# Zeros beside the low parts of the queries, and an exponential written into the tile of weights

## The chip, the core and the metric

The kernel runs on one core of a Trainium2 chip. A core has five engines, each with an instruction queue of its own that it works through in order: TensorE (PE in the profile, its weight loads are PEld), VectorE (DVE), ScalarE (ACT), GpSimd (POOL) and SyncE (SP, which issues the DMAs). They wait for each other by semaphores. The metric is the device time of one launch in microseconds, the median of some runs. Beside the times there is one profiled execution, whose trace has every instruction with its start and its duration.

## The reference

Two layers over 528 positions (16 learned ones ahead of 512) and 1024 channels in float32. The first is a Hyena mixer (long convolutions), the second a differential attention with 16 heads; each ends with a norm and a residual. The change lies in the second. Cut to what matters:

```python
def diff_attention_mixer(h, w_in, lam_vecs, subln, w_out, cos, sin, layer_idx):
    u = h @ w_in
    # q, k: (B, T, 16 heads, 2 maps, 64), turned by the rotary tables; v: (B, T, 16, 128); z: the gate
    def attend(qb):
        s = jnp.einsum("bqhmd,bkhmd->bhmqk", qb, k).astype(F32) * scale
        p = jax.nn.softmax(s, axis=-1)
        p = p[:, :, 0] - lam * p[:, :, 1]
        return jnp.einsum("bhqk,bkhd->bqhd", p.astype(v.dtype), v)
    o = rmsnorm(o, subln, DA_NORM_EPS) * (1.0 - lam_init)
    return (o.reshape(B, T, D_INNER) * jax.nn.silu(z)) @ w_out
```

Each head has two maps of scores over 64 dimensions. Their softmaxes are subtracted, and the difference weighs the values.

## The kernel before

Float32 products are made of three: each operand is split into a high part that the fast float32 format of TensorE holds exactly and the low rest, and high x high, high x low and low x high are summed in PSUM.

**The scores of a tile.** The 512 queries of a head are four tiles of 128, so the layer has 64 tiles; I count them through, tile 0 to 63, tile 4 being the first of the second head. `scores` makes one tile. A map has 64 dimensions and the array 128 rows, so two of the three products fit into one passage: `ks[:, map]` holds the high part of the keys on its own 64 partitions and the low part on the other 64, and `qs[:, map]` holds the high part of the queries on both. One matmul of line 1302 for each half of the 528 keys (264 columns) makes high x high and high x low. The third product, low queries x high keys, is line 1306: `ql` holds the low parts of map 0 on partitions 0 to 63 and of map 1 on 64 to 127, and each matmul takes the 64 partitions of its map alone. So a tile has four matmuls of line 1302 and four of line 1306. A map's scores lie in a PSUM tile `a` of two banks, of which there are two.

**From scores to weights.** Line 1309 is VectorE's maximum over the 528 scores of a query, line 1311 ScalarE's exponential with its sum. Both exponentials go to tiles `E`, of which there are three. Line 1317 is VectorE's sum `E0 - factor x E1` into the tile of weights `pp`. There are eight of these, four for a head. Line 1318 is a copy by GpSimd of the weights of the 16 learned positions, line 1327 the transposes of the weights (four transposes of 128 keys for each of four tiles of keys, and one group with 96 columns for the 16 learned positions), lines 1348 to 1352 weights x values. The pool of `pp` also serves the first layer's result, which `turn_back` (line 966) copies out of PSUM and sends to DRAM at the start of the attention for the last residual.

**What sets the order.** `attend` writes the four tiles of scores of a head and, between them, the transposes and weighted values of the head before. Between those it issues steps of a list of projections (`Filler`): keys, queries, values and gates of later heads (lines 345, 348 and 1189) and output projections of earlier ones (line 1237). A scheduler then puts each engine's instructions into a final order by a simulated timeline of its own, so the order on the engines is not that of the source. The reading of tile buffers (pools with a number of buffers) sets further waits: whoever writes a buffer waits for the last reader of what was in it. `q_split` (line 1139) makes `qs` and `ql` out of a head's turned queries.

Of the kernel before, what the change touches and what calls it, by code (L numbers as in the profile page):

```python
# [10 lines left out]
F32 = mybir.dt.float32  # L11
F32R = mybir.dt.float32r
I32 = mybir.dt.int32
AF = mybir.ActivationFunctionType
# [5 lines left out]
P = 128  # L20
# [16 lines left out]
# ---------------------------------------------------------------- host side  # L37
# [95 lines left out]
# -------------------------------------------------------------- device side  # L133
# [7 lines left out]
class Item:  # L141
    """one projection: its weight tiles in DRAM, and its steps as (cost, body)"""
# [5 lines left out]
class Filler:  # L148
    """Steps of projections in their order; they are issued between the steps of the chains that
    would leave the tensor engine waiting, their weights one item ahead."""  # L150
# [42 lines left out]
class Trunk:  # L193
# [20 lines left out]
    def rsqrt(self, dst, src, scale, eps, n, rows=P):  # L214
        """dst = (src * scale + eps) ** -0.5 on small tiles."""
# [17 lines left out]
    def root(self, dst, src, scale, eps, n, rows=P):  # L233
        """dst = (src * scale + eps) ** -0.5 by the square root of ScalarE and one step of Newton's"""
# [13 lines left out]
    def token_rms(self, part, tiles, scale=1.0 / D, how=None):  # L248
        """1/rms of tiles of tokens, from sums of squares over the channels: one column for each tile"""
# [25 lines left out]
    def diagonals(self, r, j, n, m, dg=None):  # L275
        """columns j to j + n of r on the diagonals of square tiles"""
# [7 lines left out]
    def spread(self, dg, out):  # L284
        """diagonals as rows on every partition"""
        self.nc.tensor.matmul(out, self.ones[:dg.shape[0], :], dg, start=True, stop=True)

    def rows(self, r, j, n, m, out):
        """columns j to j + n of r, one after the other, as a row on every partition"""
# [33 lines left out]
    def wtile(self, src, eng=None, at=None):  # L323
        """one [128, 1024] weight tile from DRAM, as its two float32r parts"""
# [11 lines left out]
    def project(self, ps, wt, first, part):  # L336
        """half of one weight tile's rows against the tokens from first on: [128 columns, tokens]"""
# [12 lines left out]
    def project_part(self, out, wt, first):  # L350
        """one weight tile against the tokens from first on that out has columns for"""
# [7 lines left out]
    # ------------------------------------------------------------------ hyena  # L359
    def hyena(self):  # L360
# [5 lines left out]
        with ExitStack() as cx:  # L366
# [7 lines left out]
            # ---- transform tables  # L374
# [71 lines left out]
    def first_load(self, pf, fill):  # L446
        """the input's columns times the gain of the first norm as the operand, and the sums of their squares"""
# [22 lines left out]
    def first_norm(self, pf, rb, part):  # L470
        """1/rms of the input, by token on every partition"""
# [55 lines left out]
    def sine_layer(self, pool, ps, dst, fb, col, rows):  # L527
        """dst = sin(freq * (ps + b)), the argument brought into [-pi, pi] first"""
# [50 lines left out]
    def filter_net(self, pf, hs, t):  # L579
        """the filters' network, one layer at a time"""  # L580
# [13 lines left out]
    def filters(self, ph, hs, hb, dtl, rnt, dpf, dpb, hsp, run):  # L594
        """the filters, their sums over the lags, and their transforms, 256 channels at a time"""
# [19 lines left out]
        # ---- sums over lags, and the taps that wrap  # L615
# [19 lines left out]
    def taps(self, ph, c, hs, part):  # L635
        """forward plus and minus backward taps: in [lag, channel], and the last lags in [channel, lag]"""
# [74 lines left out]
    def long_conv(self, pb, c, st, vb, nb, ib, rnt, dpf, dpb, hsp, skip, vn, run, need):  # L711
# [7 lines left out]
        # ---- fold, and turn to [time, channel]  # L719
# [33 lines left out]
        # ---- forward transform, product with the filters  # L753
# [33 lines left out]
        # ---- back to time: P from (Zr even, Zi odd), Q from (Zr odd, Zi even)  # L787
# [41 lines left out]
    def out_item(self, c, st, before):  # L829
        """output projection of one chunk, summed over the chunks; of the last ones by half of the tokens"""  # L830
# [11 lines left out]
    def out_half(self, sts, ws, dt, h):  # L842
        """one tile of channels, for half of the tokens, of one or two chunks"""
# [26 lines left out]
    # --------------------------------------------------- between the two layers  # L870
    def boundary(self, pa, pb):
        """h1 = x + norm(y), and its norm, half of the tokens after the other"""
# [13 lines left out]
        def square(part, src, k, sl, engs):  # L886
            """squares, summed over the even and the odd tiles of channels"""
# [82 lines left out]
    def attention(self):  # L970
        tc, nc, I = self.tc, self.nc, self.I
        v, g, s, te = nc.vector, nc.gpsimd, nc.scalar, nc.tensor
        with ExitStack() as cx:
# [15 lines left out]
            for i, e in ((0, v), (1, g)):  # L989
                e.tensor_tensor(rope[:, i], rope[:, i], self.rb, op=ALU.mult)  # L990
# [408 lines left out]
```

## Time and profile before

| | us |
|---|---|
| median of 3 runs | 1459.31 |
| lowest and highest | 1457.16, 1459.79 |
| span of the profiled execution | 1454.5 |
| TensorE busy | 1382.3 (95%) |
| VectorE busy | 1128.7 (78%) |
| ScalarE busy | 741.5 (51%) |
| GpSimd busy | 521.4 (36%) |

The first layer takes about the first 690 us, a boundary between the layers follows until about 760, then the attention. The span runs from the program's first instruction to the end of its last, and is 4.8 us shorter than the median; a start and an end outside the program's instructions lie between them. Busy times are unions of instructions that may overlap. A matmul's duration in the trace holds its way through the array, most of which overlaps with the next one; how many matmuls the array takes in a time is read from the distance between their starts.

### The profile page before, as it was taken

Reading aid. Unit: us, or ns where it says so; the run is one execution under the profiler, and the core shown is the slowest. Engines: PE = TensorE matmul, PEld = TensorE weight load, DVE = VectorE, ACT = ScalarE, POOL = GpSimd, SP = SyncE. Lnnn points to the kernel's source line nnn. Section 1 sums busy time; section 2 is a strip of 40 time slices with the busy share of each in tenths; the row PEclk is TensorE's granted clock in tenths of the full one; section 3 lists DMA queues with packets and bytes.
Section 4 is the critical chain, followed back from the end, with each engine's and each line's share of the span. In section 5 each row is a group of like instructions: output and inputs, shape, how many; then the busy total and the mean of one; then the engine's idle time right before and its main releaser. Section 6 shows DMA issues by size and latency. Waiting matters only on the chain. (4 is left out here: it accounts for less than half of the span.)

```text
span 1454.5 us, 24759 instructions
## 1 busy us (share of the span) xinstructions
PE 1382.3 (95%) x9296; PEld 1259.1 (87%) x9296; DVE 1128.7 (78%) x2191; ACT 741.5 (51%) x1405; POOL 521.4 (36%) x539
## 2 busy tenths in 40 slices
PE   6889999999999999999897999999999999999994
PEld 5889899999999999999886888888888888888883
DVE  8789988877777777777758477878778787877888
ACT  5455442433333333333556677556566665657652
POOL 6367625432323232314424233223242322324223
PEclk9999999999999999999898999999999999999997
DMA  6343432132222222224211312212021221202211
GB/s 211 106 135 125 154 135 84 62 117 88 87 88 88 88 87 88 87 88 148 65 42 44 102 44 73 71 46 73 30 87 59 73 68 49 73 30 87 87 66 58
DMA packets 63560, 123.48 MB, mean 85 GB/s; under 512 B 7297, under 2 KB 11649, under 8 KB 63441
## 3 DMA queue, kind: packets, MB, share of 16 engines
q1 hardware_dynamic: 63440, 121.91, 25.5%
q8 instruction: 73, 1.20, 0.3%
q14 instruction: 47, 0.38, 0.1%
HBM read 109.30 MB, written 12.58 MB: 84 GB/s over the span
## 5 line engine op out<-in xcount | busy, mean ns | idle before, releaser
L209 ACT CAST wh<-wr 128x512 fp32r<-128x512 f32 x314 | 181.7, 618 | 247.6 <-PE b L348 69.4
L348 PE MATMUL b<-xh,wh 128*128 128x264 f32 x1024 | 265.2, 292 | 2.8 <-ACT wh L209 0.9
L348 PE MATMUL b<-xl,wh 128*128 128x264 f32 x1024 | 263.7, 290 | 2.6 <-DVE xl L458 2.6
L348 PE MATMUL b<-xh,wl 128*128 128x264 f32 x1024 | 258.7, 289 | 1.2 <-POOL wl L212 1.2
L212 DVE TENSOR_TENSOR wl<-wr,wh 128x512 fp32r<-128x512 f32 x250 | 184.3, 764 | 28.2 <-ACT wh L209 25.3
L348 PEld LDWEIGHTS b<-xh,wh 128*128 128x128 f32 x1024 | 184.3, 193 | 6.5 <-ACT wh L209 1.7
L348 PEld LDWEIGHTS b<-xl,wh 128*128 128x128 f32 x1024 | 183.9, 192 | 4.3 <-DVE xl L458 3.5
L348 PEld LDWEIGHTS b<-xh,wl 128*128 128x128 f32 x1024 | 181.8, 193 | 1.7 <-POOL wl L212 1.5
L212 POOL TENSOR_TENSOR wl<-wr,wh 128x512 fp32r<-128x512 f32 x64 | 95.7, 1514 | 88.5 <-ACT wh L209 88.5
L1309 DVE TENSOR_REDUCE mx<-a 128x1 f32<-128x528 f32 x128 | 89.4, 700 | 24.2 <-PE a L1306 23.8
L1311 ACT ACTIVATE E<-a,mx 128x528 f32<-128x528 f32 x128 | 89.6, 701 | 30.1 <-DVE mx L1309 15.3
L345 PE MATMUL b<-xh,wh 128*128 128x512 f32 x232 | 95.1, 410 | 0.0
L345 PE MATMUL b<-xl,wh 128*128 128x512 f32 x232 | 92.1, 397 | 0.0
L345 PE MATMUL b<-xh,wl 128*128 128x512 f32 x232 | 91.9, 396 | 0.0
L1167 POOL TENSOR_TENSOR ro<-ro,rope 128x528 f32<-128x528 f32 (+1 forms) x32 | 42.6, 1332 | 121.6 <-ACT ro L1161 121.4
L1189 PE MATMUL b<-wh,xh 128*128 128x256 f32 x256 | 75.8, 296 | 6.8 <-DVE vl L1199 6.0
L514 POOL TENSOR_SCALAR u<-vecs 128x1 f32<-128x1 f32 x96 | 26.3, 294 | 151.9 <-DVE cv L519 133.7
L1252 DVE SCALAR_TENSOR_TENSOR acc<-b,rh,acc 128x512 f32<-128x512 f32 x96 | 70.2, 742 | 6.8 <-PE b L1237 6.0
L1189 PE MATMUL b<-wl,xh 128*128 128x256 f32 x256 | 72.9, 285 | 0.0
L1189 PE MATMUL b<-wh,xl 128*128 128x256 f32 x256 | 72.9, 285 | 0.0
L1318 POOL COPY pp<-pp 128x80 f32<-128x80 f32 x64 | 17.9, 280 | 149.6 <-DVE pp L1317 145.0
L1306 PE MATMUL a<-ks,ql 64*128 64x264 f32 x256 | 67.6, 341 | 0.0
(380 smaller groups left out, 3986.6 us busy)
## 6 DMA issues: line engine op xcount, KB each, us to landing
wr<-in_w_in SPq DMA_DIRECT2D x128, 256.0 KB, 2.8
wr<-in_w_out SPq DMA_DIRECT2D x64, 256.0 KB, 2.9
hsp<-ho SPq DMA_DIRECT2D x16, 512.0 KB, 2.7
H<-hsp SPq DMA_DIRECT2D x16, 512.0 KB, 3.9
wr<-in_w_k SPq DMA_DIRECT2D x32, 256.0 KB, 2.7
wr<-in_w_q SPq DMA_DIRECT2D x32, 256.0 KB, 2.6
wr<-in_w_z SPq DMA_DIRECT2D x32, 256.0 KB, 2.6
wr<-in_w_v SPq DMA_DIRECT2D x32, 256.0 KB, 2.7
```

Of the source, the lines that this page charges most:

```text
L209: self.nc.scalar.copy(dst, src)
L212: (eng or self.nc.vector).tensor_tensor(dst, src, hi.bitcast(F32), op=ALU.subtract)
L345: te.matmul(ps, w[:, wk], x[:, k, first:T], start=st, stop=sp)
L348: te.matmul(ps[h], w[:, wk], x[:, k, h * TH:(h + 1) * TH], start=st, stop=sp)
L514: g.tensor_scalar(u[:, e:e + 1], b_in[:, mt:mt + 1], -1.0, None, op0=ALU.mult)
L1167: g.tensor_tensor(y, y, rope[:, 1, n0:n0 + n], op=ALU.mult)
L1189: te.matmul(ps[:n, :256], x, wv[k // 4][w][:, wk], start=(k == 0 and q == 0), stop=(k == KT - 1 and q == len(ops) - 1))
L1252: self.nc.vector.scalar_tensor_tensor(y, ps, r, y, op0=ALU.mult, op1=ALU.add)
L1306: te.matmul(pss[mp][:, h, :TH], ql[own, tq], ks[own, mp, h * TH:(h + 1) * TH], start=False, stop=True)
L1309: v.tensor_reduce(mx, ps[:, :, :TH], axis=AX.XY, op=ALU.max, negate=True)
L1311: s.activation(r2(e), ps[:, :, :TH], AF.Exp, bias=mx, accum_out=s0[:, qt:qt + 1] if mp == 0 else sm[:, 0:1])
L1318: self.nc.gpsimd.tensor_copy(view(p, 0, [META, 5], [1, META]), view(p, MR - META, [0, 5], [1, META]))
```

## The change

The docstrings and comments go, which moves line numbers and nothing else. In the code, three things change.

- The low parts of the queries lie in two fixed tiles `qlo0` and `qlo1` (for even and odd heads) with a plane for each map, 128 partitions by two maps by 512. Map 0's low parts stand on partitions 0 to 63 of plane 0, map 1's on 64 to 127 of plane 1, and the other halves are set to zero once, by four memsets of GpSimd at the start of the layer. Line 1306 (1311 after the change) then takes all 128 partitions of `ql[:, map]` and `ks[:, map]`: the zeros meet the low parts of the keys. `ql` before was a tile of the pool with two buffers, written by the same two subtractions.
- These matmuls are written map by map, both halves of the keys of one map after each other.
- The tile `pp` is taken at the start of `scores`, the first map's exponential writes into it, and the sum is made in place. `E` has two buffers instead of three and holds the second map's exponential alone.

```diff
+            self.qlo = [self.tl(k1, [P, 2, S], F32R, f"qlo{i}") for i in (0, 1)]
+            for t in self.qlo:
+                g.memset(t[0:64, 1].bitcast(F32), 0.0)
+                g.memset(t[64:P, 0].bitcast(F32), 0.0)
...
-            lv = self.tl(pc, [P, 4, 64], F32, "E", bufs=3)
+            lv = self.tl(pc, [P, 4, 64], F32, "E", bufs=2)
...
-        ql = st["ql"] = self.tl(pc, [P, S], F32R, "ql", bufs=2)
+        ql = st["ql"] = self.qlo[st["h"] % 2]
         a, b = slice(0, 64), slice(64, P)
         self.hi(qs[a, 0], o[a])
         self.hi(qs[b, 1], o[b])
-        self.lo(ql[a], o[a], qs[a, 0])
-        self.lo(ql[b], o[b], qs[b, 1])
+        self.lo(ql[a, 0], o[a], qs[a, 0])
+        self.lo(ql[b, 1], o[b], qs[b, 1])
...
-        es = []
+        p = self.tl(pc, [P, MR + S], F32, "pp", bufs=8)
+        es = [p[:, MR - META:], self.tl(pc, [P, T], F32, "E", bufs=2)]
...
-        for h in (0, 1):
-            for mp in (0, 1):
-                own = slice(64 * mp, 64 * mp + 64)
-                te.matmul(pss[mp][:, h, :TH], ql[own, tq], ks[own, mp, h * TH:(h + 1) * TH], start=False, stop=True)
+        for mp in (0, 1):
+            for h in (0, 1):
+                te.matmul(pss[mp][:, h, :TH], ql[:, mp, tq], ks[:, mp, h * TH:(h + 1) * TH], start=False, stop=True)
...
-            e = self.tl(pc, [P, T], F32, "E", bufs=3)
-            s.activation(r2(e), ps[:, :, :TH], AF.Exp, bias=mx,
+            s.activation(r2(es[mp]), ps[:, :, :TH], AF.Exp, bias=mx,
                          accum_out=s0[:, qt:qt + 1] if mp == 0 else sm[:, 0:1])
-            es.append(e)
...
-        p = self.tl(pc, [P, MR + S], F32, "pp", bufs=8)
-        v.scalar_tensor_tensor(p[:, MR - META:], es[1], sm[:, 2:3], es[0], op0=ALU.mult, op1=ALU.add)
+        v.scalar_tensor_tensor(es[0], es[1], sm[:, 2:3], es[0], op0=ALU.mult, op1=ALU.add)
```

The scheduler lays the attention out anew. Up to the first scores TensorE's order is the same; behind them it differs in places. The first place is TensorE at the first tile of the eighth head (tile 28). `a` are the score tiles in PSUM, `qs` and `ql` (`qlo`) the high and low queries, `b<-ident,pp` the transposes of the last 96 columns of weights of the sixth head, `b<-gh,wh` an output projection. A row that ends in x2 stands for two matmuls into the same tile, one for each half of the keys. Before:

```order
L1237 MATMUL b_12330<-wh_12236,gh_11895 128x512
L1237 MATMUL b_12330<-wl_12237,gh_11895 128x512
L1237 MATMUL b_12330<-wh_12236,gl_11896 128x512
L1302 MATMUL a_12489<-ks_12066,qs_12175 128x264 x2
L1306 MATMUL a_12489<-ks_12066,ql_12176 128x264 x2
L1327 MATMUL b_12339<-ident_66,pp_11548 96x128
L1327 MATMUL b_12339<-ident_66,pp_11659 96x128
L1327 MATMUL b_12339<-ident_66,pp_11748 96x128
L1327 MATMUL b_12339<-ident_66,pp_11827 96x128
L1189 MATMUL b_12350<-wh_12121,xh_81 128x256
```

After the change:

```order
L1242 MATMUL b_12300<-wh_12207,gh_11870 128x512
L1242 MATMUL b_12300<-wl_12208,gh_11870 128x512
L1242 MATMUL b_12300<-wh_12207,gl_11871 128x512
L1308 MATMUL a_12461<-ks_12040,qs_12148 128x264 x2
L1311 MATMUL a_12461<-ks_12040,qlo_1477_9113 128x264 x2
L1308 MATMUL a_12462<-ks_12040,qs_12148 128x264 x2
L1311 MATMUL a_12462<-ks_12040,qlo_1477_9113 128x264 x2
L1329 MATMUL b_12309<-ident_66,pp_11507 96x128
L1329 MATMUL b_12309<-ident_66,pp_11617 96x128
L1329 MATMUL b_12309<-ident_66,pp_11704 96x128
L1329 MATMUL b_12309<-ident_66,pp_11782 96x128
```

The scores of the tile's second map, which stood behind 27 matmuls of projections, now follow those of the first map at once, and the transposes come behind both.

The second place is ScalarE at the start of the attention, from the second exponential of tile 2 on. `E_...` and `pp_..., s` or `sm` are exponentials with their sums; `COPY pp<-b` are the copies of the first layer's result that `turn_back` makes. Before:

```order
L1311 ACTIVATE E_9410,sm_9393<-a_9395,mx_9408 128x528
L1311 ACTIVATE E_9486,s_1497_9187<-a_9474,mx_9484 128x528
L1311 ACTIVATE E_9490,sm_9473<-a_9475,mx_9488 128x528
L1311 ACTIVATE E_9708,s_1583_9685<-a_9696,mx_9706 128x528
L966 COPY pp_9575<-b_9570 128x512
L966 COPY pp_9593<-b_9588 128x512
L966 COPY pp_9601<-b_9596 128x512
L966 COPY pp_9609<-b_9604 128x512
L1311 ACTIVATE E_9712,sm_9695<-a_9697,mx_9710 128x528
L966 COPY pp_9617<-b_9612 128x512
```

After the change:

```order
L1315 ACTIVATE E_9396,sm_9397<-a_9399,mx_9411 128x528
L1315 ACTIVATE pp_9474,s_1498_9192<-a_9477,mx_9487 128x528
L966 COPY pp_9575<-b_9570 128x512
L966 COPY pp_9593<-b_9588 128x512
L966 COPY pp_9601<-b_9596 128x512
L966 COPY pp_9609<-b_9604 128x512
L1315 ACTIVATE E_9475,sm_9476<-a_9478,mx_9490 128x528
L966 COPY pp_9617<-b_9612 128x512
L966 COPY pp_9625<-b_9620 128x512
L966 COPY pp_9633<-b_9628 128x512
L966 COPY pp_9641<-b_9636 128x512
L1315 ACTIVATE pp_9695,s_1579_9685<-a_9698,mx_9708 128x528
```

The first four copies moved ahead of the second exponential of tile 3, and both exponentials of tile 4, which stood ahead of the second four copies, moved behind them.

On GpSimd two of the four memsets stand ahead of the first, and two ahead of the second of the two subtractions of line 212 that follow each other at the end of the first layer (688.6 and 693.3 us in the trace).

## Rows read from the trace of the kernel before

**Rows 1.** Page, busy us, share of the span, instructions.
```profile
PE 1382.3 (95%) x9296; PEld 1259.1 (87%) x9296; DVE 1128.7 (78%) x2191; ACT 741.5 (51%) x1405; POOL 521.4 (36%) x539
```

**Rows 2.** Busy time by stretch of the span, columns in the first row.
```profile
core 0: us, PE busy (x) PEld busy (x) DVE busy (x) ACT busy (x) POOL busy (x), PEclk, DMA share, GB/s
...
760.00:800.00 40.00, 29.34 (x174) 25.23 (x173) 31.98 (x48) 27.41 (x61) 18.12 (x14) 0.83 0.17 53
800.00:1400.00 600.00, 599.86 (x3516) 509.74 (x3515) 461.75 (x926) 385.57 (x761) 187.71 (x181) 1.00 0.21 66
```

**Rows 3.** Waits of TensorE, 776 to 1410 us: total us, times, longest us.
```profile
PE a L1302 <- ACT E L1311: 2.2, 3, 0.9
PE b L963 <- DVE vh L1199: 1.0, 1, 1.0
PE b L963 <- DVE vl L1199: 0.7, 1, 0.7
```

**Rows 4.** Groups by form, 760 us on: busy us, mean ns of one.
```profile
L1306 PE MATMUL a<-ks,ql 64*128 64x264 f32 x256 | 67.6, 341 | 0.0
```

**Rows 5.** TensorE in order of time: start us, us, what. A whole pair.
```profile
1129.11 0.40 PE L1302 MATMUL a<-ks,qs 128*128 128x264 f32 x2
1129.44 0.51 PE L1306 MATMUL a<-ks,ql 64*128 64x264 f32 x2
1129.88 0.50 PE L1348 MATMUL b<-ph,vh 96*128 96x512 f32 x1
1130.21 0.40 PE L1237 MATMUL b<-wh,gh 128*128 128x512 f32 x1
1130.45 0.40 PE L1237 MATMUL b<-wl,gh 128*128 128x512 f32 x1
...
1130.92 0.41 PE L348 MATMUL a<-xh,wh 128*128 128x264 f32 x2
1131.16 0.28 PE L348 MATMUL a<-xl,wh 128*128 128x264 f32 x1
```

**Rows 6.** TensorE in order of time: one half of a torn pair.
```profile
1090.63 0.39 PE L1237 MATMUL b<-wh,gl 128*128 128x512 f32 x1
1090.95 0.38 PE L1306 MATMUL a<-ks,ql 64*128 64x264 f32 x1
1091.26 0.50 PE L1348 MATMUL b<-ph,vh 96*128 96x512 f32 x1
1091.60 0.40 PE L1237 MATMUL b<-wh,gh 128*128 128x512 f32 x1
```

**Rows 7.** ScalarE in order of time, seventh head; idle time before in brackets.
```profile
1029.95 0.70 ACT L1311 ACTIVATE E<-a,mx 128x528 f32<-128x528 f32 x1
...
1039.47 0.70 ACT L1311 ACTIVATE E<-a,mx 128x528 f32<-128x528 f32 x1 [1.29 <-DVE pp L1317]
```

**Rows 8.** TensorE in order of time, the same stretch.
```profile
1031.96 0.41 PE L1302 MATMUL a<-ks,qs 128*128 128x264 f32 x2
...
1033.77 0.40 PE L1302 MATMUL a<-ks,qs 128*128 128x264 f32 x2
...
1039.35 0.41 PE L1302 MATMUL a<-ks,qs 128*128 128x264 f32 x2
...
1040.12 0.64 PE L1327 MATMUL b<-ident,pp 128*96 128x128 f32 x4
```

**Rows 9.** Groups by form: idle us before them, and what ended it.
```profile
L1311 ACT ACTIVATE E<-a,mx 128x528 f32<-128x528 f32 x128 | 89.6, 701 | 30.1 <-DVE mx L1309 15.3 <-DVE pp L1317 10.0 <-DVE i L1374 1.9
```

**Rows 10.** ScalarE, then VectorE, in order of time, tile 4.
```profile
805.01 2.06 ACT L966 COPY pp<-b 128x512 f32<-128x512 f32 x4 [2.22 <-PE b L963]
...
807.85 0.77 DVE L1317 SCALAR_TENSOR_TENSOR pp<-E,sm,E 128x528 f32<-128x528 f32 x1 [4.60 <-DMA h1d<-pp]
```

**Rows 11.** GpSimd in order of time: program start, end of first layer.
```profile
0.71 0.20 POOL masks.py:197 MEMSET ident<- 128x128 f32 x1 [0.29 <-POOLq L1391]
...
693.27 1.29 POOL L212 TENSOR_TENSOR Zl<-wr,Zl 128x512 fp32r<-128x512 f32 x1 [3.42 <-ACT Zl L209]
```

## The prediction

> **What bounds the kernel now.** I read the busy line of the page first, then the busy time of each engine by stretch, then the list of waits with TensorE as the one that waits, and only then single instructions in order of time. The busy line gives TensorE 95% of the span and VectorE 78% [rows 1]. The stretches tell where that matters: from 800 to 1400 us, which is the attention layer from its second head to its last, TensorE is busy 599.86 of 600 us at a granted clock of 1.00, VectorE 461.75 and ScalarE 385.57 [rows 2]. From 760 to 800 us, where the first head begins, TensorE is busy 29.34 of 40 us only [rows 2]. The list of waits confirms it: between 776 and 1410 us TensorE waits five times, 3.9 us in all [rows 3]. So in this layer the end is set by TensorE's own row of instructions, and one microsecond that leaves that row is nearly one that leaves the time, as long as the others still deliver in time. A busy TensorE is not one at its peak, though: ends of matmuls are modelled, so I go by starts.
>
> **The third product: what it costs now.** There are 256 matmuls of line 1306, on 64 rows of the array [rows 4], in 64 tiles of queries times two maps, two halves of the keys each. TensorE's order has them as pairs, both of one map, so both on the same half of the array's rows. A whole pair is in [rows 5]. Two matmuls of 264 columns on 128 rows take 0.24 us from start to start (line 348, 1130.92 to 1131.16). The two of line 1302 ahead of the pair take 0.33 until the pair starts (1129.11 to 1129.44), 0.09 more. The pair itself takes 0.44 (to 1129.88), 0.20 more. The next matmul, of 512 columns, takes 0.33 (to 1130.21) where the one after it takes 0.24: 0.09 more. Together 0.38 us a pair that the columns do not explain. I read it as the array finishing what is in it each time the number of rows changes, and as the second matmul's weights not being loaded behind the first matmul.
> Six of the 128 pairs are torn apart by other work (maps of tiles 17, 24, 32, 40, 48 and 56). One such single matmul is in [rows 6]: 0.32 before it instead of 0.24, 0.31 after it instead of 0.12, 0.34 for the next instead of 0.24, so 0.37 each.
> With 128 rows, line 1306 becomes a matmul of the form of line 1302 with the same moving operand, for which this trace has 0.12 us. Gone are then 122 x 0.38 + 12 x 0.37 = 46.4 + 4.4 = 50.8 us of TensorE's row. The zeros cost nothing: 64 or 128 rows, the 264 columns pass once. Were a matmul beside zeros a little dearer, say 0.01 us, it would be 256 x 0.01 = 2.6 us less; were it cheaper, nothing speaks for that.
>
> **What does not come through.** First, tiles 0 to 4 (ten pairs) lie before 800 us, where TensorE waits for ScalarE anyway. Of 0.38 us there only what stands ahead of the maximum, about half, is on the chain; for the other half I take off 10 x 0.2 = 2 us. Second, the other engines. TensorE's row from 800 to 1400 shrinks by some 48 to about 552 us, and VectorE's 461.75 are then 84% of it instead of 77%, ScalarE's 385.57 70%. Neither is the bound by its sum, but both work in order. A place that has little to spare: the exponential of the first map of a tile ends at 1029.95 + 0.70 = 1030.65, and the next tile's scores, which take its PSUM buffer, start at 1031.96 [rows 7, 8]: 1.3 us to spare. What lies between does not shrink on ScalarE, but TensorE will arrive there two or three pairs, 0.8 to 1.1 us, earlier. That still fits, barely; with VectorE's queue fuller I take 0.4 us a head as lost, over 15 heads 6 us. The bounds are nothing, and 1.5 us a head (23 us).
>
> **The exponential in the tile of weights.** No instruction comes or goes: the same two exponentials, maxima and the same sum over 528 columns, now in place. What moves are waits. The first map's exponential no longer takes one of the three E buffers, so the second map's waits no longer for the sum of the tile before, but for that of the tile before it. ScalarE waited 10.0 us on such sums in the whole layer [rows 9]; one is the exponential at 1039.47, which waited 1.29 us [rows 7], and its scores had started at 1033.77 [rows 8]. It can now run some 2 us earlier, and the scheduler uses it: it pulls the second map of a head's first tile up to the first one. For TensorE that is worth nothing, because it didn't wait there.
> In return the exponential must find its tile of weights free, where before only VectorE's sum had to. There are eight such tiles, four a head; a head's first one is free once the weights of two heads before are turned, the last of them by the four transposes at 1040.12, which follow the scores of 1039.35 [rows 8]. The maximum and the cast of the transposed tile come in between on the same engines, so ScalarE would have been there no sooner: nothing. Once it is different. The rows kept for the end of the kernel pass through the same eight tiles at the start; VectorE's sum of tile 4 waited 4.60 us for such a DMA until 807.85, after ScalarE's second four copies from 805.01 [rows 10]. Now ScalarE waits in its place, with both exponentials of tile 4 behind the copies in its order, and the projection of the third head's keys behind those. But the first four copies now stand two exponentials earlier in its order, and TensorE has 24 matmuls of 512 columns (24 x 0.235 = 5.6 us) ahead of that projection. I take 2 us lost, between nothing and 5.
>
> **The zeros.** Four memsets of 64 x 512 on GpSimd come ahead of and between two subtractions of line 212. The nearest row is one of 128 x 128 on the same engine, 0.20 us [rows 11]; by columns that is 0.8 each, 3.2 in all. GpSimd stood idle 3.42 us before the second of these subtractions [rows 11], and two of the memsets come ahead of the first. I take nothing, with this idle time as the cover; without it 3.2 us.
>
> **Sum.** 50.8 - 2 - 6 - 2 = 40.8 us. The profiled execution has a span of 1454.5, 4.8 below the median of 1459.31; 1454.5 - 40.8 = 1413.7, and with these 4.8 us 1418.5. I say 1418. Everything before 690 us is in the same order as before and stays.
>
> **Rivals.**
> B, VectorE and ScalarE set the pace: each head loses 1.5 us more than it has to spare, 16 x 1.5 = 24 us of the 50.8, with the 4 us above: 1459.3 - 22.8 = 1436.5. For it: VectorE at 84%, and 1.3 us to spare at one place in every second head. Against it: from 776 to 1410 us TensorE waited three times for ScalarE and twice for VectorE, none longer than 1.0 us [rows 3].
> C, the two matmuls of a pair use the halves of the array side by side, and the 0.44 us after the pair's start are a wait of the next matmul that stays. Then a pair's two passages would take the array 0.12 us now and 0.24 after the change, and only 0.09 + 0.09 - 0.12 = 0.06 us a pair would be won: 128 x 0.06 = 7.7, less the 2 at the start, 1454. Against it: the 0.44 stands behind whole pairs whatever comes next, and TensorE's order has no two neighbours on different halves. The Trainium skill, TensorE: Matmul & The Clock Gate, Part 3 (packing small matmuls), has it that matmuls on different groups of rows run at once, with starts some 4 ns apart, which speaks for leaving 64 rows alone; by that rule the sum would be these 7.7 us, by the row it is 50.8, and the row decides.
> D, slower: the exponential waits for its tile of weights in every head, not once. Its price is the wait that VectorE had for such a tile, 4.60 us [rows 10], 16 times: 73.6 - 50.8 = 23 us more, 1482. It decides once a head loses over 3.2 us (50.8 / 16). Against it: the transposes come within 0.8 us of the scores [rows 8].
> E, the change doesn't do what it says: the 0.38 us come with the change of operands, not of rows, and stay. Then only the waits are left: 1461. Against it: within line 348 operands change as well, from xh to xl, and it takes 0.24 [rows 5].
>
> **How the numbers follow.** Chances: my forecast 0.72 (1407 to 1428), B 0.18 (1428 to 1445), C 0.02, D 0.04, E 0.04. About 0.2% (2.9 us) is what a measurement of this kernel tells from no change. Forecast, B and C are faster by more than that: 0.92; E is within it: 0.04; D slower: 0.04. The low end is the whole 50.8 us and one more, 1407; the high end takes in rival B's middle, 1438.
>
> **What would show it.** In the profile after, line 1311 should have 256 matmuls on 128 rows, a pair 0.24 us from start to start, with 0.24 before and after. TensorE should have waits of some 6 to 10 us between 776 and 1370 us, by ScalarE's exponentials or VectorE's evictions. A wait of ScalarE for the DMA of the kept rows should stand near 805 us. Wrong would be a pair that still takes 0.4 us, or waits of TensorE of over 1 us in every head.

## The result, and the profile after

The changed kernel takes 1431.97 us (median of four runs, 1428.67 to 1433.15) beside 1459.05 for the kernel before on the same chip: a ratio of 0.9815, 95% interval 0.9801 to 0.9829, 27.1 us less. The forecast was 1418, 41 us less. The profiled execution has a span of 1430.4 us, 24.1 less than the 1454.5 of before. In every run on record a launch takes 1.7 to 2.2 us longer than its span, so of the 4.8 us between the median and the span of the kernel before some 2 lie outside the program's instructions; the rest says that its profiled execution was one of its shortest. That is also why the spans differ by 24.1 us and the medians by 27.1.

The busy line of the page after, which answers to [rows 1]: TensorE is busy 43 us less, each of the others within 6 us of before.

```profile
PE 1339.1 (94%) x9296; PEld 1244.2 (87%) x9296; DVE 1134.2 (79%) x2191; ACT 738.0 (52%) x1405; POOL 519.3 (36%) x543
```

Busy time by stretch, as [rows 2]; the columns are the stretch, its length, the busy time of TensorE, its weight loads, VectorE, ScalarE and GpSimd with their instructions, the granted clock, and the DMA's share and GB/s. The attention's steady part now ends at 1376 instead of 1400 us.

```profile
core 0: us, PE busy (x) PEld busy (x) DVE busy (x) ACT busy (x) POOL busy (x), PEclk, DMA share, GB/s
760.00:800.00 40.00, 29.79 (x191) 27.36 (x192) 32.38 (x48) 29.62 (x63) 17.85 (x15) 0.83 0.21 77
800.00:1376.00 576.00, 558.07 (x3485) 495.27 (x3484) 466.54 (x922) 377.36 (x750) 182.84 (x180) 0.99 0.21 66
```

TensorE was busy 599.86 of 600 us there [rows 2]; now it stands 17.9 of 576 us idle. The list of its waits from 776 to 1390 us says on whom (total us, times, longest), and answers to [rows 3]:

```profile
PE b L1242 <- DVE zg L1224: 7.8, 5, 1.6
PE b L345 <- DVE acc L1257: 7.0, 5, 1.6
PE a L1308 <- ACT pp L1315: 2.1, 2, 1.3
```

The first two are five places each, one of each in every second head, of up to 1.6 us. All waits of the list from 776 us on come to 21.1 us; it was 3.9 [rows 3].

The third product itself is as forecast. TensorE in order of time, the changed counterpart of [rows 5]:

```profile
1107.98 0.40 PE L1242 MATMUL b<-wh,gl 128*128 128x512 f32 x1
1108.22 0.40 PE L1308 MATMUL a<-ks,qs 128*128 128x264 f32 x2
1108.46 0.41 PE L1311 MATMUL a<-ks,qlo 128*128 128x264 f32 x2
1108.70 0.42 PE L1308 MATMUL a<-ks,qs 128*128 128x264 f32 x2
1108.96 0.41 PE L1311 MATMUL a<-ks,qlo 128*128 128x264 f32 x2
```

Scores on 128 rows, the third product beside zeros, the second map's scores, its third product: 0.24 to 0.26 us from each to the next, and 0.24 before the first. The 0.09 before, 0.20 within and 0.09 behind a pair [rows 5] are gone.

For the account of the 24.1 us I take the first and the last third product, which the summary of one line's instructions gives (shortest, median and longest in ns, first and last start in us). Of the kernel before, then of the changed one:

```profile
L1306 PE MATMUL a<-ks,ql x256: 275/383/587, 776.3 to 1405.3; 64*128 64x264 f32 x128
```

```profile
L1311 PE MATMUL a<-ks,qlo x256: 279/284/425, 774.6 to 1384.5; 128*128 128x264 f32 x128
```

The layers ahead take 1.7 us less (776.3 to 774.6; no instruction of TensorE, VectorE or ScalarE moved there, so I take that for a spread between executions). From the first to the last third product it is 609.9 us instead of 629.0, 19.1 less, where the forecast's sum was 40.8. What follows the last one takes 45.9 instead of 49.2, 3.3 less: 15 matmuls that stood behind the last third product stand ahead of it now, some 2.5 us by the distances between starts of their shapes. So the missing part lies between the first and the last third product, and its largest waits come in every second head.

One of these places, tiles 30 to 32. TensorE: scores of tile 31 at 1061.17, the last of the gate's projection (line 345) from 1061.67, then the output projection (line 1242), which has to wait for the PSUM buffer that the gate's projection filled:

```profile
1061.17 0.41 PE L1308 MATMUL a<-ks,qs 128*128 128x264 f32 x2
...
1061.67 0.39 PE L345 MATMUL b<-xh,wl 128*128 128x512 f32 x1
...
1064.72 0.39 PE L1242 MATMUL b<-wh,gl 128*128 128x512 f32 x1
1066.68 0.50 PE L1242 MATMUL b<-wh,gh 128*128 128x512 f32 x1 [1.57 <-DVE zg L1224]
...
1070.23 0.51 PE L345 MATMUL b<-xh,wh 128*128 128x512 f32 x1 [1.60 <-DVE acc L1257]
```

The buffer is free when VectorE has read it (line 1224). VectorE's own order of the same time:

```profile
1061.45 0.70 DVE L1314 TENSOR_REDUCE mx<-a 128x1 f32<-128x528 f32 x1
1063.01 0.16 DVE L1317 RECIPROCAL sm<-sm 128x1 f32<-128x1 f32 x1 [0.86 <-ACT E L1315]
...
1063.34 0.74 DVE L1257 SCALAR_TENSOR_TENSOR acc<-b,rh,acc 128x512 f32<-128x512 f32 x1
1064.00 1.41 DVE L1319 SCALAR_TENSOR_TENSOR pp<-E,sm,pp 128x528 f32<-128x528 f32 x1
1065.33 0.69 DVE L1314 TENSOR_REDUCE mx<-a 128x1 f32<-128x528 f32 x1
1065.95 0.67 DVE L1224 TENSOR_TENSOR zg<-b,rb 128x512 f32<-128x512 f32 x1
```

The gate's projection had been complete since about 1062.1, but VectorE read it at 1065.95. Ahead of it in the queue stood the reciprocal of tile 30, which waited 0.86 us for ScalarE's exponential, then an accumulation, tile 30's whole sum over 528 columns (1064.00, 1.41 us), and the maximum of tile 31, 4.2 us behind its scores. The row is the same at all five places. The sum itself is long there: its median is 0.77 us, and beside this one GpSimd worked on two subtractions of line 212 (1063.56, 2.98 us). The 49 sums of the changed kernel that overlap no work of GpSimd take at most 0.77 us, and all eight that take more than 1 us overlap some; others overlap it and stay at 0.77. What this adds to a stall was not tested by itself.

### The profile page after: what moved, and what is told of

It is laid out like the page before. It is cut to its first block, busy times and chain, and to the rows that moved or that the text cites. A ratio compares the mean times of both kernels' runs of the same rounds, so it can differ in the third digit from the quotient of the medians.

```text
span 1430.4 us, 24734 instructions
## 1 busy us (share of the span) xinstructions
PE 1339.1 (94%) x9296; PEld 1244.2 (87%) x9296; DVE 1134.2 (79%) x2191; ACT 738.0 (52%) x1405; POOL 519.3 (36%) x543
## 5 line engine op out<-in xcount | busy, mean ns | idle before, releaser
L1257 DVE SCALAR_TENSOR_TENSOR acc<-b,rh,acc 128x512 f32<-128x512 f32 x96 | 70.7, 742 | 24.1 <-PE b L1242 23.4
L209 ACT CAST ph<-b 128x512 fp32r<-128x512 f32 (+1 forms) x80 | 46.7, 586 | 30.4 <-PE b L1329 29.9
L502 DVE TENSOR_TENSOR u<-b,rb 128x264 f32<-128x264 f32 x96 | 38.4, 423 | 28.8 <-PE b L348 27.5
```

The costliest lines, as they stand in the source:

```text
L209: self.nc.scalar.copy(dst, src)
L502: v.tensor_tensor(dst[:, sl], ps[h], self.rb0[:, sl], op=ALU.mult)
L1257: self.nc.vector.scalar_tensor_tensor(y, ps, r, y, op0=ALU.mult, op1=ALU.add)
```

## The experiments

Theory O: the loss comes with the new order of instructions that the scheduler makes once the first exponential goes into the tile of weights. Rival R: VectorE cannot follow a shorter TensorE row in any order. Rival W: the sharing of the tile of weights costs by its own waits. From e9 on, theory V: the stalls are VectorE being late, and go with its load; rival Q: the sequence alone counts. The scheduler lays the order out for each kernel anew, so an edit can change two things at once; what a comparison of the traces says of the order stands with each run. The table has what was measured of each run: the median; its ratio to the kernel before on the same chip with the 95% interval; from the profiled execution, the time from the first to the last third product, and TensorE's waits from 800 to 1376 us in all.

```
run                            us        ratio (interval)          first to last   waits
before                         1459.05   -                         629.0            0.9
changed                        1431.97   0.9815 (0.9801, 0.9829)   609.9           17.0
e1 zeros, old order            1418.22   0.9730 (0.9714, 0.9745)   590.9            6.8
e2 exponential alone           1465.07   1.0048 (1.0031, 1.0066)   638.3            4.8
e3 changed, old loops          1439.21   0.9876 (0.9857, 0.9895)   612.5           16.3
e4 changed, gate low on GpSimd 1436.74   0.9851 (0.9832, 0.9871)   617.0           18.7
e5 zeros, old order, new loops 1419.43   0.9726 (0.9706, 0.9745)   592.1            6.5
e6 zeros, two E                1443.11   0.9894 (0.9880, 0.9909)   623.4           23.5
e7 changed, one E              1428.09   0.9787 (0.9765, 0.9809)   603.3           11.8
e8 changed, again              1431.89   0.9822 (0.9801, 0.9842)   611.4           15.3
e9 changed, half maxima        1419.46   0.9729 (0.9709, 0.9750)   597.7            9.5
e10 e5 with half maxima        1420.15   0.9740 (0.9721, 0.9759)   599.7            9.5
e11 before, half maxima        1453.07   0.9959 (0.9946, 0.9972)   629.9            0.6
e12 changed, gate by ScalarE   1440.73   0.9879 (0.9848, 0.9909)   612.6           16.7
```

**e1, the zeros alone, in the order of before.** Three E tiles and separate tiles of weights again; two tiles gl (the low parts of the gated values) instead of three make room. The instructions of TensorE, VectorE and ScalarE stand in the order of the kernel before, one for one. Against the changed kernel:

```diff
-        p = self.tl(pc, [P, MR + S], F32, "pp", bufs=8)
-        es = [p[:, MR - META:], self.tl(pc, [P, T], F32, "E", bufs=2)]
+        es = []
...
-        for mp in (0, 1):
-            for h in (0, 1):
+        for h in (0, 1):
+            for mp in (0, 1):
...
-            s.activation(r2(es[mp]), ps[:, :, :TH], AF.Exp, bias=mx,
+            e = self.tl(pc, [P, T], F32, "E", bufs=3)
+            s.activation(r2(e), ps[:, :, :TH], AF.Exp, bias=mx,
...
+            es.append(e)
...
-        gl = self.tl(pc, [P, S], F32R, "gl", bufs=3)
+        gl = self.tl(pc, [P, S], F32R, "gl", bufs=2)
```

> The low parts beside zeros alone, in the order of the kernel before: the exponentials have three tiles of their own and the sum writes the weights, as before, and the loop over the halves stays outside; the 4 KB of zeros are paid for by two tiles gl instead of three. TensorE's, VectorE's and ScalarE's instructions then stand exactly as in the kernel before. Theory O (the order): the 24 us that the prediction missed are lost by the new order, in which the exponential into the tile of weights lets the second map of a head's first tile come right behind the first; then this kernel takes 1416 to 1423. Theory R (VectorE's rate): with TensorE's row 50 us shorter VectorE cannot follow in any order; then 1428 to 1438, with waits of TensorE for VectorE of 15 us or more between 776 and 1390 us.

1418.22 us, 40.3 below the kernel before. Busy time from 800 to 1376 us (columns as above) and TensorE's waits there:

```profile
800.00:1376.00 576.00, 569.14 (x3594) 510.68 (x3594) 469.10 (x947) 393.59 (x773) 195.08 (x185) 1.00 0.22 71
```

```profile
PE b L1242 <- DVE acc L1257: 4.6, 5, 1.0
...
PE b L1242 <- DVE vl L1204: 0.9, 1, 0.9
```

VectorE does 469 us in this stretch, more than the 467 of the changed kernel, because more of the layer fits into it, and TensorE waits for it 5.5 us, not 16.5. R falls: VectorE can follow. VectorE's row at the place shown above, in this order:

```profile
1057.86 0.16 DVE L1318 RECIPROCAL sm<-sm 128x1 f32<-128x1 f32 x1 [1.31 <-ACT E L1315]
1058.43 1.89 DVE L1321 SCALAR_TENSOR_TENSOR pp<-E,sm,E 128x528 f32<-128x528 f32 x1
...
1062.27 0.71 DVE L1313 TENSOR_REDUCE mx<-a 128x1 f32<-128x528 f32 x1
1063.01 0.75 DVE L1257 SCALAR_TENSOR_TENSOR acc<-b,rh,acc 128x512 f32<-128x512 f32 x1
1063.68 0.70 DVE L1313 TENSOR_REDUCE mx<-a 128x1 f32<-128x528 f32 x1
1064.29 0.68 DVE L1224 TENSOR_TENSOR zg<-b,rb 128x512 f32<-128x512 f32 x1
1064.89 0.15 DVE L1318 RECIPROCAL sm<-sm 128x1 f32<-128x1 f32 x1
1064.96 0.73 DVE L1257 SCALAR_TENSOR_TENSOR acc<-b,rh,acc 128x512 f32<-128x512 f32 x1
```

The second maximum of tile 30, the first of tile 31 and the gate's read (1064.29) come ahead of the reciprocal (1064.89) and the sum of tile 30. VectorE waits for an exponential here too, and as long in all: from 800 to 1376 us its reciprocals wait 14.4 us in e1 and 14.1 in the changed kernel. But here that wait and the long sum behind it (tile 29) are over at 1060.32, before the last matmul of the gate's projection starts (1061.11); in the changed kernel they stand between the projection and its read.

**e2, the exponential alone,** on the kernel before, with its products on 64 rows:

```diff
-        es = []
+        p = self.tl(pc, [P, MR + S], F32, "pp", bufs=8)
+        es = [p[:, MR - META:], self.tl(pc, [P, T], F32, "E", bufs=2)]
...
-            e = self.tl(pc, [P, T], F32, "E", bufs=3)
-            s.activation(r2(e), ps[:, :, :TH], AF.Exp, bias=mx,
+            s.activation(r2(es[mp]), ps[:, :, :TH], AF.Exp, bias=mx,
```

> The first exponential written into the tile of weights alone, on the kernel before: two E tiles, the low parts of the queries on 64 rows as before. It has the new order of instructions without the shorter row of TensorE. Theory O: the new order costs by itself where TensorE has little to spare, so 1462 to 1480, with waits of TensorE for VectorE of 1 us and more in every second head. Theory R: at the old row VectorE still follows, whatever the order; 1456 to 1461.

1465.07, 6.5 us slower than before (4.5 to 9.6 by the interval). On TensorE, VectorE and ScalarE its order is that of the changed kernel except around the last tile. TensorE's waits, 800 to 1376 us:

```profile
PE b L345 <- DVE acc L1252: 4.5, 5, 1.4
```

The second place of the changed kernel is there already, at the old row's pace: the projection's buffer behind VectorE's accumulations, once in every second head. Only one of the five is over 1 us, where theory O had each so. Shown: this half of the change costs by itself, and it costs more when TensorE's row is shorter (e3 less e1, the same loops: 21 us).

**e3, the old loops in the changed kernel** (halves of the keys outside, maps inside, as the third hunk of e1).

> The changed kernel with the two loops around the third product exchanged back (halves of the keys outside, maps inside). If TensorE's order has them as pairs of one map anyway, both theories expect 1430 to 1434, no difference from the changed kernel; a difference of over 3 us would say that the loop order is a third part of the change, with a price of its own.

1439.21, 7 us above the changed kernel, which neither theory had. TensorE's order differs around the last tile alone. What follows the last third product takes 49.4 us in this profile and 45.9 in that of the changed kernel: 3.5 of the 7. The rest is not in these profiles: e3's profiled execution is its shortest (1435.10 us), only 2.9 us above that of the changed kernel. e5 below says whether the loops cost the same in another order.

**e4, the low parts of the gate's weights on GpSimd,** one argument of the gate's item:

```diff
-        return Item([self.I["w_z"][st["h"]]], [...], self.nc.vector)
+        return Item([self.I["w_z"][st["h"]]], [...], self.nc.gpsimd)
```

> The changed kernel with the low parts of the gate's weights (two subtractions of line 212 a head, 0.77 us each on VectorE) moved to GpSimd, which is busy a third of the time. VectorE is relieved by 1.5 us a head, some 23 us in all. Theory R: TensorE's waits for VectorE shrink by about the relief where it binds, so 1412 to 1424. Theory O: the load in sum is not what counts; within 5 us of the changed kernel, 1427 to 1437, unless the order happens to move the two places.

1436.74, 5 us slower than the changed kernel, though VectorE has 1.5 us less in each head; TensorE's waits are 18.7 us. R's 1412 to 1424 fails a second time, and O's 1427 to 1437 just holds. The order was laid anew here too, so the run does not say what the relief is worth by itself.

**e5, e1 with the loops of the change.**

> The zeros in the order of the kernel before (as e1), with the loop over the maps outside, as the change has it. The instructions stand on each engine in the order of e1. If the loop's order is worth the 7 us by which e3 was behind the changed kernel, wherever it is used, this takes 1409 to 1413; if it only moved the order at the end of e3, 1416 to 1420.

1419.43: the loops make no difference in this order, and the time of e1 repeats on another chip. So e3's 7 us are no price of the loops as such.

**e6, the zeros with two E tiles,** both exponentials in them, the sum into the tile of weights as before:

```diff
-            e = self.tl(pc, [P, T], F32, "E", bufs=3)
+            e = self.tl(pc, [P, T], F32, "E", bufs=2)
...
-        gl = self.tl(pc, [P, S], F32R, "gl", bufs=2)
+        gl = self.tl(pc, [P, S], F32R, "gl", bufs=3)
```

(against e1)

> The zeros, both exponentials in E tiles and the sum into the tile of weights as before, but with two E tiles in place of three (and three tiles gl again), the old loops. This has a third order of instructions, neither that of before nor that of the changed kernel. Theory O (the order sets the time): another time than both, I cannot say on which side; over 3 us from 1418 and with TensorE's waits for VectorE at places of its own. Rival W (writing into the tile of weights is what costs, by its waits): nothing is written there early here, so 1416 to 1421.

1443.11, the slowest of the kernels with zeros, and nothing is shared in it. TensorE's waits, 800 to 1376 us, then ScalarE's exponentials (busy us, mean ns of one, idle us before them and what ended it):

```profile
PE b L345 <- DVE acc L1257: 8.1, 6, 1.8
PE b L1194 <- DVE pl L212: 5.5, 6, 1.1
PE b L1242 <- DVE acc L1257: 5.0, 5, 1.7
```

```profile
L1315 ACT ACTIVATE E<-a,mx 128x528 f32<-128x528 f32 x128 | 89.6, 701 | 73.5 <-DVE pp L1321 64.0
```

The places are others (line 1194, the values' projection, behind a low part of VectorE's). But this is no run of the order alone: with two E tiles for both maps ScalarE waited 64.0 us for VectorE's sums, where the kernel before has 10.0 [rows 9]. W's 1416 to 1421 is missed, and what settles W is the trace of the changed kernel: from 776 to 1390 us ScalarE waited for no tile of weights and for no E tile there.

**e7, the changed kernel with one E tile.**

```diff
-        es = [p[:, MR - META:], self.tl(pc, [P, T], F32, "E", bufs=2)]
+        es = [p[:, MR - META:], self.tl(pc, [P, T], F32, "E", bufs=1)]
```

> The changed kernel with one E tile in place of two: the second map's exponential again waits for the sum of the tile before, as it did in the kernel before with its three tiles, and cannot be pulled up; the first is still written into the tile of weights. Theory O: most of what the new order lost comes back, 1417 to 1425. Rival W: the loss is in the waits for the tile of weights and stays, 1430 to 1440.

1428.09, between the two: 4 us better than the changed kernel by medians, with the intervals overlapping, and 10 behind e1. The order is neither that of before nor that of the changed kernel. TensorE's waits for the accumulations at line 345 are gone, those for the gate's read are not (9.1 us). O's 1417 to 1425 was missed: one of the two places is gone in this order, the other has grown.

**e8, the changed kernel again.**

> The changed kernel itself beside the others on their chip, for the size of its distance from e5 to e7 and from e3: 1429 to 1434 by its first measurement; if it comes out at 1436 or more, e3's 7 us were a difference of chips.

1431.89: the first measurement stands.

**e9, e10, e11, maxima over half of the keys,** in the changed kernel, in e5 and in the kernel before:

```diff
-            v.tensor_reduce(mx, ps[:, :, :TH], axis=AX.XY, op=ALU.max, negate=True)
+            v.tensor_reduce(mx, ps[:, 0, :TH], axis=AX.X, op=ALU.max, negate=True)
```

> The changed kernel with each maximum taken over the first half of the keys only (264 of 528 columns; left out is the other half, and the exponentials' common factor with it, which the norm takes out again). It takes some 0.3 us off each of 128 maxima on VectorE, 35 us between 800 and 1376 us, and nothing off TensorE; the scheduler's order moves with it. Theory V (TensorE's stalls are VectorE being late, so they go with VectorE's load): TensorE's waits for VectorE in this stretch fall from 15 us to under 6, and the time to 1411 to 1420. Theory Q (the sequence alone counts, whatever VectorE's load): another order, another time, 1425 to 1440.

> The zeros without the exponential in the tile of weights (e5), each maximum over the first half of the keys only. Theory V: the 5 waits of TensorE for VectorE's accumulation that e5 kept (4.3 us) go, 1408 to 1415. Theory Q: not below e5's 1419 by more than 3 us.

> The kernel before with each maximum over the first half of the keys only: the control, VectorE relieved where TensorE's row is still the long one. TensorE had one stall there, so theory V says 1457 to 1461, no difference; a gain of over 4 us would say that shorter maxima help by something else than the stalls.

A maximum takes 0.425 us instead of 0.699. All three have orders of their own. e9: 1419.46, 12.5 below the changed kernel. Its busy time and waits, 800 to 1376 us:

```profile
800.00:1376.00 576.00, 565.90 (x3555) 502.33 (x3554) 432.29 (x943) 385.10 (x763) 191.47 (x183) 1.00 0.21 67
```

```profile
PE b L1329 <- DVE acc L1257: 5.0, 5, 1.0
PE b L1242 <- DVE acc L1257: 1.8, 3, 1.2
PE b L1242 <- DVE zg L1224: 1.1, 5, 0.2
```

VectorE has 34 us less there. The time is V's, the waits (9.5, of them 9.3 for VectorE) are not under 6, and they moved to other places. e10: 1420.15, no gain over e5, against V's 1408 to 1415. Its largest wait:

```profile
PE b L1331 <- DVE acc L1257: 5.0, 5, 1.0
```

That is e9's first wait (the line is 1329 there) and not one of e5's: the order of e10 is not e5's but nearly that of e9, with the same order on GpSimd. So neither run holds an order still and relieves VectorE alone. What they show is that two kernels of nearly one order take nearly one time, 1419.46 and 1420.15, with the first exponential in the tile of weights and without; how much of e9's 12.5 us is the shorter maximum and how much the new order stays open. e11: 1453.07, 6 us below the kernel before, where V said none and took more than 4 us for a sign of something else than stalls. From the first to the last third product nothing is won (629.9); 3.3 us are in what follows the last (45.9 for 49.2). The two profiled executions are only 1.4 us apart, so the rest is not in these profiles.

**e12, the gate's projection copied by ScalarE.**

```diff
-        self.nc.vector.tensor_tensor(z, ps, self.rb[:, META:], op=ALU.mult)
+        self.nc.scalar.copy(z, ps)
+        self.nc.vector.tensor_tensor(z, z, self.rb[:, META:], op=ALU.mult)
```

> The changed kernel with ScalarE copying the gate's projection out of its PSUM buffer (one more instruction a head there), and VectorE's multiplication reading the copy: the buffer that the output projection waits for in every second head no longer comes free in VectorE's queue, whose load stays. Theory V (TensorE's stall there is that buffer held behind VectorE's queue): the 5 waits for the gate's tile, 7.8 us, are gone, and 1421 to 1427 if nothing takes their place. Theory Q: some 200 of TensorE's rows stand elsewhere, so that other waits may come up and the time lands anywhere from 1428 to 1440, with no waits for the gate's tile either.

1440.73, above V's 1421 to 1427 and just above Q's 1428 to 1440. TensorE's waits, 800 to 1376 us, then ScalarE in order of time at the same place as above:

```profile
PE b L1243 <- ACT zg L1224: 9.2, 5, 1.9
```

```profile
1064.88 1.13 ACT L209 CAST wh<-wr 128x512 fp32r<-128x512 f32 x2
1065.91 2.53 ACT L209 CAST qs<-ro 64x512 fp32r<-64x512 f32 x4
1068.34 0.57 ACT L1224 COPY zg<-b 128x512 f32<-128x512 f32 x1
```

The five waits stayed, with another name, which neither theory had; the order was laid anew here too. The copy, 0.57 us, stands in ScalarE's queue behind two casts of weights and four of queries, 3.5 us from start to start. That corrects theory V: the wait does not belong to VectorE, it comes with the place in an engine's queue of the read that frees the buffer.

## Why the prediction was right about the sign and 14 us off

**What bounds the kernel, and the 50.8 us.** Right to 2 us. e1 and e5 do the first half of the change alone and come out 40.3 and 40.2 us below the kernel before; the sum for that half, without the 2 us for the DMA, was 50.8 - 2 - 6 = 42.8. As e1 has TensorE's order of before, the two can be laid beside each other matmul by matmul: the distances between starts that the sum counts, around the third products, are 48.8 us shorter where neither kernel waits. The term of 6 us lost to the other engines is the size of e1's waits (6.8 for 0.9 before), but that is partly luck: it was worked out at the PSUM buffer that ScalarE's exponential frees, and 5.5 of the 6.8 us are waits for VectorE, 1.3 for ScalarE. The Trainium skill, TensorEngine Tiling (Array Packing), Key Properties, has it that a change of tiling mode drains TensorE; the trace fits that, the 0.09 us on either side of a pair [rows 5] are gone with the 64 rows. Rival C (7.7 us won) and rival E (nothing won) fall by the same runs; the side-by-side start of small matmuls that C took from the Trainium skill, TensorE: Matmul & The Clock Gate, Part 3, could not appear here, as no two neighbours were on different halves.

**The exponential in the tile of weights: the step that failed.** The prediction saw that the scheduler would pull a second map up, counted it as worth nothing because TensorE had not waited there, and charged 2 us for a DMA. It measured +6.5 us alone (e2) and +12.5 to +13.7 beside the zeros (changed and e8, less e1 and e5). The working looked only at the instruction that was moved and at what it had waited for. What had to be read, in the order of the changed kernel, is what then stood behind it on VectorE: a reciprocal that waits for an exponential and a whole sum, with a maximum and the gate's read queued after them. Without the 2 us for the DMA the sum gives 1416.5; that is the time of the half that was understood (e1: 1418.22). That the forecast of 1418 is e1's time almost to the digit, and not the changed kernel's, says how much the other half was left out.

**The start.** Wrong, by the DMA: a wait of ScalarE for it was to stand near 805 us. ScalarE's copies of the kept rows and the exponential of tile 4 in the changed kernel:

```profile
794.98 2.04 ACT L966 COPY pp<-b 128x512 f32<-128x512 f32 x4
...
797.71 2.67 ACT L966 COPY pp<-b 128x512 f32<-128x512 f32 x4
800.47 0.70 ACT L1315 ACTIVATE pp<-a,mx 128x528 f32<-128x528 f32 x1
```

The exponential follows the second four copies without a wait, and neither ScalarE nor VectorE waited for that DMA anywhere from 776 to 830 us; VectorE's 4.60 us [rows 10] went away instead of moving.

**The zeros.** Right that they cost nothing. The last of the four memsets and the subtraction after it:

```profile
690.59 0.52 POOL L995 MEMSET qlo<- 64x512 f32 x1
691.97 1.28 POOL L212 TENSOR_TENSOR Zl<-wr,Zl 128x512 fp32r<-128x512 f32 x1 [0.85 <-ACT Zl L209]
```

0.52 us, not 0.8, and GpSimd still waits 0.85 before the subtraction, of the 3.42 it had [rows 11].

**Rival B** had the time (1436.5, within 1428 to 1445) and not the cause. VectorE at 81% was no bound: e1 has it at 81% too, with 6.8 us of waits. And the largest waits are at two places in every second head, not 1.5 us in each head. **Rival D** did not occur; ScalarE waited for no tile of weights.

**What would show it.** The third product came as written. TensorE's waits were to be 6 to 10 us and are 21; waits of over 1 us in every head were named as the sign of being wrong, and they came in every second. The measured 1431.97 lies outside the forecast's own stretch (1407 to 1428, chance 0.72) and in that of rival B (0.18). That the range, 1407 to 1438, held it is luck as far as the mechanism goes: the high end was set by rival B's middle.

The Trainium skill, Perfetto Trace Analysis, Optimization Strategies, says to optimize the engines that the waiting matmul engine is blocked by. Here that did not serve as a rule for choosing: with less work on VectorE the time fell by 12.5 us in e9, not at all from e5 to e10, and rose by 5 in e4; with one read taken over by ScalarE it rose by 9 in e12; and the old order with separate tiles won 13 with VectorE's load as it was. The order was new in the first four, so no run here tests the rule by itself.

From the first to the last third product the changed kernel takes 19.0 us longer than e1. TensorE's waits there make 9.9 of them (22.0 for 12.0, those before 800 us included). Stopping and starting again make some 4.3: the matmul before a wait stands with its whole 0.39 us and the first one behind it takes 0.34 until the next, both instead of 0.23, and the waits are 30 for 14. The 15 matmuls that stand ahead of the last third product only in the changed kernel make some 2.5, and come back in the 3.3 us that it takes less behind it. The other 2 us are spread over the stretch. These are sums over two single executions.

Open: no run has the changed kernel's order with separate tiles, so that the order and not the sharing costs rests on the traces, where ScalarE waits for no shared tile, and on e12. Whether an order better than that of before exists was not tried: no order was written out by hand.

## What to carry to other kernels

When buffers or their sharing change under a scheduler that lays the order itself, price the whole new order: go through the queue of each engine that frees TensorE's buffers, and look for instructions that wait for a third engine between the moment when a buffer is ready to be read and the read that frees it. Separate the halves of a change before shipping both: here the first half alone, in the order of before, beats both kernels (e1, 1418.22), and the second costs a third of its gain. The same work, in different orders and with different numbers of buffers, took 1418 to 1443 us here (e1, e6).

## What the hardware showed that was not expected

After short stalls TensorE's granted clock can fall. Busy time and granted clock (third column from the end) in the changed kernel at another of its places:

```profile
976.00:980.00 4.00, 4.00 (x21) 3.06 (x19) 3.10 (x6) 2.81 (x6) 3.88 (x4) 1.00 0.17 66
980.00:984.00 4.00, 2.47 (x11) 2.09 (x11) 3.94 (x7) 2.69 (x6) 1.71 (x2) 0.78 0.42 131
984.00:988.00 4.00, 3.39 (x10) 2.38 (x9) 3.90 (x8) 2.06 (x5) 0.00 (x0) 0.50 0.00 2
988.00:992.00 4.00, 4.00 (x17) 3.23 (x16) 0.99 (x3) 0.00 (x0) 0.26 (x1) 0.87 0.00 0
```

TensorE had been busy for all of the 4 us before 980, then waited 1.5 and 0.6 us, and the granted clock went from 1.00 to 0.50 (1.2 of 2.4 GHz) and back to 1.00 by 992. Clock times time, that is at most 0.22 x 4 + 0.50 x 4 + 0.13 x 4 = 3.4 us; what fell into a wait cost nothing. At 1064 to 1070, after waits of 1.6 and 1.6 us, it stayed at 1.00. In e8, the same kernel, three places give 6.8 us together, and yet its profiled span (1428.9) is 1.5 us shorter; so executions of one kernel differ by it, and no run here shows what it adds to the time. It does not explain the distance to e1: from the first to the last third product the clock stood at 0.50 for 13.7 us in both, in e1 from 789 to 803 us, in the changed kernel from 788 to 795 and from 982 to 989. The prediction had no such term.
